# A decoder layer of Trainium2: the order of its first transfers and products, where its resident weights land, and what paces the mixers' steps

## The chip, the cores and the metric

The kernel runs on one core of one Trainium2 chip. The metric is device time in microseconds (us) of that core, as the median of several runs. Beside it stands one profiled execution, which the trace describes instruction by instruction.

## The reference

One layer of a decoder trunk, for 256 tokens (T), a width D of 2048 and a batch of 1, all in float32:

```python
mod = silu(c) @ w_ada + b_ada                    # 6 x D: shift, scale, gate of both halves
h = rmsnorm(x) * (1 + sc1) + sh1
proj = h @ w_in                                  # pool u | q,k,v | gla q,k,v,r,a | 3 x D gate logits
y_pool = pool(u); y_sb = stick_breaking(q, k, v) # 4 windows; 8 heads of 128
y_gla = gla(...)                                 # 4 heads, decay from a
y = sum_i sigmoid(g_i) * (y_i @ w_br_i)
x = x + ga1 * (y @ w_out)
h = rmsnorm(x) * (1 + sc2) + sh2
x = x + ga2 * ((silu(h @ w_gate) * (h @ w_up)) @ w_down)
```

## The kernel before

Everything is held transposed: channels on the 128 partitions, tokens along the free axis, so D is 16 blocks of 128. A tile framework puts in the semaphores and chooses, from its own estimates, the order in which each engine's instructions are issued; instructions may move ahead of earlier ones unless an edge forbids it.

**Products.** Matmuls run on float32r operands. A float32 factor is split into a rounded float32r part, hi, and a rest, lo: ACT casts hi (L113), DVE subtracts to get lo (L114), in parts of `PART` = 1024 columns (768 for some). `mm3` makes hi·hi, hi·lo and lo·hi (L128 to L130); token-major pieces do the same at L342. A plain float32 product is two passes of the array and far slower per column; it is used where an operand isn't split (L309, the mixers, the start).

**Buffers.** `wraw` has four raw buffers of 128 x 2048 float32 (`raw`), into which SP loads, in one queue, everything heavy: weights (`load`, L94) and rows of w_ada (`ada_vec`, L227). `wsplit` has three buffers for hi and lo. `slots` has 61 tiles of 128 x 512 float32 (`slot`) for everything else. PSUM has four banks `acc` and four `mx`.

**Vectors.** A column of `mod` is the dot product of c and a 1 MB block of w_ada: `ada_vec` lets DVE multiply and add (L230) against `cs`, which is silu(c) spread over all partitions by four products (L215) with a one-hot matrix `oh`.

**Stage 1, start.** SP loads x in four tiles, ACT squares them, PE sums them over partitions by `c2048` products (L267), and `rsqrt` gives rstd. `keep_busy` (L206) runs products of zeros.

**Stage 2, blocks 0 to 15.** As soon as block n of h is known (`modulate`, two vectors a block), PE applies `persistent(n)`, 12 products into six resident banks (the first three head pairs' q and k), in plain float32 for n < 5 (L309) from weights in slots, and through `Weights` behind that; and `extra`, pieces of the other 16 column pairs for some blocks of h, each summed into a slot by ACT or DVE (L320, L322). From block 4 on every block has two such pieces of 1 MB.

**Stage 3, mixers.** 33 short chains (generators `stick_breaking`, `gla_level`, `pool` and so on) are advanced in steps between the last pieces and then the gate projections (`gate`, `proj`: 48 of them, 48 products each). `steps(n)` advances up to n of the chains that are due by a `clock` that each call moves by a fixed cost; 30 gates (`LEAD`) come before the merge. `ada(n)` adds n to a running count and computes one vector for every 2 in it.

**Stage 4.** The merge of the branches, w_out, the second norm and SwiGLU, with `mm2` (a 512 and a 256 column product, L147, L148).

Of the kernel before, what the change touches and what calls it, by code (L numbers as in the profile page):

```python
# [8 lines left out]
F32 = mybir.dt.float32  # L9
# [5 lines left out]
P = 128  # L15
# [43 lines left out]
def kernel(ctx: ExitStack, tc: tile.TileContext, xT, c, vecs, consts, invc, masks, w_ada, w_per, w_ext,  # L59
                      w_gate, w_a1, w_a2, w_pool, w_br, w_out, w_ff, w_down, outT):  # L60
    nc = tc.nc
    mm = nc.tensor.matmul
    recent = deque(maxlen=6)
# [6 lines left out]

    vec = nc.vector

# [18 lines left out]
    def load(src):  # L91
        raw = wraw.tile([P, WW], F32, tag="raw", name=f"raw{next(names)}")
        n = src.shape[-1]
        nc.sync.dma_start(raw[:, :n], src)  # L94
        return raw[:, :n]

    def split_buffer(shift, n):
        t = wsplit.tile([P, 2 * PART + 128], F32R, tag="w", name=f"w{next(names)}")
        return t[:, shift:shift + n], t[:, shift + PART:shift + PART + n]

    class Weights:

        def __init__(self, src, part=PART, shift=SHIFT):
            self.raw, self.part, self.shift, self.made = load(src), part, shift, {}

        def at(self, col, n):
            i = col // self.part
            if i not in self.made:  # L110
                raw = self.raw[:, i * self.part:min((i + 1) * self.part, self.raw.shape[-1])]
                hi, lo = split_buffer(self.shift, raw.shape[-1])
                nc.scalar.copy(hi, raw)  # L113
                vec.tensor_tensor(lo, raw, hi.bitcast(F32), ALU.subtract)  # L114
# [75 lines left out]
    cz, oh, idle = slot()[:4, :], slot()[:4, :], slot()  # L190
    nc.scalar.dma_start(cz, c[0])
    nc.scalar.dma_start(oh, c[1])
    nc.scalar.preload_act_table_set("silu_and_others")
    vec.memset(idle, 0.0)
    for i in range(4):
        nc.sync.dma_start(xt[i], xT[:, 4 * i:4 * i + 4, :])
    nc.sync.dma_start(vt, vecs)
    c2048, c128, neg, eps = full(1.0 / D), full(1.0 / P), full(-1.0), full(EPS, 1)
# [24 lines left out]
    def ada_vec(t, parts=1):  # L223
        raw = wraw.tile([P, WW], F32, tag="raw", name=f"raw{next(names)}")
        w = D // parts
        for i in range(parts):
            nc.sync.dma_start(raw[:, i * w:(i + 1) * w], w_ada[t, :, i * w:(i + 1) * w])  # L227
# [29 lines left out]
    for i in range(4):  # L257
        sq = [slot(), slot()]
        for j in range(2):
            act(sq[j], xt[i][:, 2 * j:2 * j + 2, :].rearrange("p a t -> p (a t)"), AF.Square)  # L260
        if i < 2:
            vec.tensor_copy(*spread[2 * i])
        vec.tensor_tensor(sq[0], sq[0], sq[1], ALU.add)
        if i < 2:
            nc.scalar.copy(*spread[2 * i + 1])
        for j in range(2):
            mm(ms[:, :T], lhsT=c2048, rhs=sq[0][:, j * T:(j + 1) * T], start=i == 0 and j == 0,  # L267
               stop=i == 3 and j == 1)
    keep_busy(4)
    ada_vec(16, 2)  # L270
# [27 lines left out]
    def persistent(k):  # L298

        if k < NATIVE:  # L300
            w = [slot() for _ in range(3)]
            for i, wi in enumerate(w):
                nc.sync.dma_start(wi, w_per[k, :, i * 512:(i + 1) * 512])
# [22 lines left out]
    def extra(piece, bank):  # L326

        es, c0, c1 = EXT[piece][1:]
        n = (c1 - c0) * T
        w = Weights(w_ext[piece, :, :n * len(es)], 768 if n == 768 else PART)  # L330
        for i, e in enumerate(es):
# [261 lines left out]
    live = [0, 0]  # L593
    clock = [0]
    LEAD, LIVE, LAG, ST, ST2 = 30, 5, 1, 3, 2

    def unfinished():
        return bool(chains or lines[0] or lines[1])

    def steps(n, cost=5.2):  # L600
        clock[0] += cost
        for i, line in enumerate(lines):
            while line and live[i] < LIVE:
                chains.append([0, line.popleft(), i])
                live[i] += 1
        done = 0
        for e in sorted(chains, key=lambda e: e[0]):
            if done >= n or e[0] > clock[0]:
                break
            try:  # L610
                v = next(e[1])
                e[0] = clock[0] + (1 if v == "idle" else (v or 5) * LAG)
                done += v != "idle"
            except StopIteration:
                chains.remove(e)
                done += 1
# [7 lines left out]
    raw = load(w_a1)  # L624
    hi = split_buffer(0, 768)[0]
# [22 lines left out]

    def gate(due):

# [10 lines left out]
        sigs.append(s)  # L661
        ada(due)
        if unfinished():
            steps(ST)

    for n in range(LEAD):
        gate(0 if n < 10 else 1.4)
    while unfinished():
        steps(ST)
    assert raw  # L670
# [8 lines left out]
    for j in range(NK):  # L679
        while len(sigs) < min(3 * NK, LEAD + -(-(j + 1) * (3 * NK - LEAD) // NK)):  # L680
            gate(1.3)
        sig = sigs[3 * j:3 * j + 3]
# [12 lines left out]
        merged.append(split_x(m[:, :T]))  # L695
        ada(1.3 if j < NK - 2 else 0)

# [223 lines left out]
```

## Time and profile before

| | us |
|---|---|
| median of 3 runs | 1555.23 |
| lowest, highest | 1554.32, 1555.28 |
| profiled execution, its own time | 1558.11 |
| span of its trace, first to last instruction | 1556.3 |

The granted clock of TensorE is 0.992 of the full 2.4 GHz over the span. PE is busy for 1524.4 us of it, DVE for 1134.2, ACT for 733.2; these are sums over stages with different limits, and the sections below go by stretches of time. Times in a trace count from its first instruction.

### The profile page before, as it was taken

What the parts mean: (1) busy time and instruction counts of PE and PEld (TensorE: products, weight loads), DVE (VectorE), ACT (ScalarE), POOL (GpSimd) and SP (SyncE); (2) the same over time, 40 slices, a digit from 0 to 9 for tenths busy, and PEclk for the clock granted to TensorE, in tenths of its full rate; (3) what the DMA queues carried; (4) which work ended last, traced back from release to release, by engine and by line L of the source; (5) the groups of instructions that cost most, each with busy time, mean ns of one, the idle gap of its engine ahead of it and who ended that gap; (6) DMA issues with size and microseconds to landing.
All of it is one profiled execution on the core that took longest, in us unless ns stands there. A gap on an engine that the chain in (4) does not pass through costs nothing.

```text
span 1556.3 us, 25106 instructions
## 1 busy us (share of the span) xinstructions
PE 1524.4 (98%) x10376; PEld 1399.8 (90%) x10376; DVE 1134.2 (73%) x1515; ACT 733.2 (47%) x1020; POOL 9.8 (1%) x28
## 2 busy tenths in 40 slices
PE   8999999889999999999999999999999999999999
PEld 5899999779999999999889888888888888888888
DVE  5788887996896788888999666666666555545443
ACT  4334334745566444444556444544444444433333
POOL 0000000000000000001000000000000000000000
PEclk9999999989999999999999999999999999999999
DMA  8988887544667888887875666667666555556562
GB/s 331 365 297 299 299 287 250 185 156 163 222 233 261 314 300 315 303 308 286 293 276 173 243 246 215 245 244 244 217 245 246 189 190 186 192 197 206 184 206 85
DMA packets 58882, 377.30 MB, mean 242 GB/s; under 512 B 6536, under 2 KB 9992, under 8 KB 17424
## 3 DMA queue, kind: packets, MB, share of 16 engines
q1 hardware_dynamic: 58752, 375.68, 68.1%
q8 instruction: 81, 1.33, 0.3%
q14 instruction: 33, 0.27, 0.0%
q10 hardware_dynamic: 16, 0.02, 0.0%
HBM read 373.58 MB, written 2.10 MB: 241 GB/s over the span
## 4 chain that ended last, share of the span: by engine, by line
PE 87%; DVE 6%; DMA 4%; issue 1%; ACT 1%; SPq 0%; ACTq 0%; DVEq 0%
PE acc L147 33%; PE acc L148 16%; PE acc L128 9%; PE acc L130 9%; PE acc L129 8%; DMA raw<-in_w_ada_dram 2%; DVE raw L230 2%; PE mx L342 2%; PE mx L128 1%; PE mx L130 1%; PE mx L129 1%; DVE w L114 1%; PE acc L309 1%; PE acc L752 1%; PE acc L750 1%
## 5 line engine op out<-in xcount | busy, mean ns | idle before, releaser
L114 DVE TENSOR_TENSOR w<-raw,w 128x1024 fp32r<-128x1024 f32 (+2 forms) x520 | 618.9, 1192 | 291.5 <-ACT w L113 288.0
L113 ACT CAST w<-raw 128x1024 fp32r<-128x1024 f32 (+2 forms) x520 | 531.9, 1024 | 513.2 <-PE acc L148 241.7
L147 PE MATMUL acc<-s,w 128*128 128x512 f32 x2212 | 767.0, 393 | 0.0
L148 PE MATMUL acc<-s,w 128*128 128x256 f32 x2212 | 614.5, 278 | 0.0
L147 PEld LDWEIGHTS acc<-s,w 128*128 128x128 f32 x2212 | 415.0, 188 | 95.3
L148 PEld LDWEIGHTS acc<-s,w 128*128 128x128 f32 x2212 | 415.9, 188 | 0.0
L130 PE MATMUL acc<-s,w 128*128 128x256 f32 x1224 | 344.8, 282 | 8.2 <-DVE w L114 8.2
L128 PE MATMUL acc<-s,w 128*128 128x256 f32 x1224 | 348.8, 285 | 0.2 <-DVE s L322 0.2
L129 PE MATMUL acc<-s,w 128*128 128x256 f32 x1224 | 344.2, 281 | 0.0
L130 PEld LDWEIGHTS acc<-s,w 128*128 128x128 f32 x1224 | 233.0, 190 | 9.1 <-DVE w L114 9.0
L230 DVE CUSTOM_DVE_ANT_0 raw<-raw,cs,vt 128x2048 f32<-128x2048 f32 (+1 forms) x96 | 223.1, 2325 | 16.1 <-DMA raw<-in_w_ada_dram 15.9
L128 PEld LDWEIGHTS acc<-s,w 128*128 128x128 f32 x1224 | 232.5, 190 | 1.9 <-issue 1.0
L129 PEld LDWEIGHTS acc<-s,w 128*128 128x128 f32 x1224 | 232.1, 190 | 1.4 <-issue 1.2
L66 ACT ACTIVATE s<-s 128x256 f32<-128x256 f32 (+3 forms) x169 | 84.3, 520 | 33.6 <-DVE s L792 16.2
L128 PE MATMUL mx<-s,w 128*128 128x256 f32 x312 | 88.7, 284 | 6.2 <-DVE s L322 6.2
L791 ACT COPY s<-acc 128x256 f32<-128x256 f32 x82 | 30.6, 373 | 136.1 <-PE acc L148 136.1
L129 PE MATMUL mx<-s,w 128*128 128x256 f32 x312 | 87.8, 281 | 0.0
L130 PE MATMUL mx<-s,w 128*128 128x256 f32 x312 | 87.7, 281 | 0.0
L792 DVE TENSOR_TENSOR s<-s,acc 128x256 f32<-128x256 f32 x82 | 34.5, 420 | 52.9 <-ACT s L791 52.9
L128 PEld LDWEIGHTS mx<-s,w 128*128 128x128 f32 x312 | 59.3, 190 | 7.2 <-ACT w L113 5.9
L342 PE MATMUL mx<-w,s 128*128 128x256 f32 x492 | 59.8, 280 | 4.3 <-DVE s L322 1.9
L342 PEld LDWEIGHTS mx<-w,s 128*128 128x128 f32 x492 | 57.8, 188 | 5.5 <-ACT w L113 2.4
(153 smaller groups left out, 932.6 us busy)
## 6 DMA issues: line engine op xcount, KB each, us to landing
raw<-in_w_ada_dram SPq DMA_DIRECT2D x94, 1024.0 KB, 5.1
raw<-in_w_ff_dram SPq DMA_DIRECT2D x88, 1024.0 KB, 4.9
raw<-in_w_gate_dram SPq DMA_DIRECT2D x48, 1024.0 KB, 5.0
raw<-in_w_down_dram SPq DMA_DIRECT2D x32, 1024.0 KB, 5.0
raw<-in_w_ext_dram SPq DMA_DIRECT2D x29, 1024.0 KB, 5.9
raw<-in_w_br_dram SPq DMA_DIRECT2D x16, 1024.0 KB, 5.4
raw<-in_w_out_dram SPq DMA_DIRECT2D x16, 1024.0 KB, 4.9
raw<-in_w_down_dram SPq DMA_DIRECT2D x16, 768.0 KB, 4.2
```

What stands on the lines that cost most here:

```text
L66: r = nc.scalar.activation(out, in_, func, **kw)
L113: nc.scalar.copy(hi, raw)
L114: vec.tensor_tensor(lo, raw, hi.bitcast(F32), ALU.subtract)
L128: mm(out, lhsT=wh, rhs=x[:, :T], start=first, stop=False, skip_group_check=True)
L129: mm(out, lhsT=wh, rhs=x[:, T:], start=False, stop=False, skip_group_check=True)
L130: mm(out, lhsT=wl, rhs=x[:, :T], start=False, stop=last, skip_group_check=True)
L147: mm(out, lhsT=wh, rhs=x, start=first, stop=False, skip_group_check=True)
L148: mm(out[:, :T], lhsT=wl, rhs=x[:, :T], start=False, stop=last, skip_group_check=True)
L230: vec.tensor_tensor_reduce(p, p, cs[:, i * w:(i + 1) * w], 1.0, mod_col(t) if i else vt[:, V_ADA + t:V_ADA + t + 1], ALU.mult, ALU.add, mo ...
L342: mm(o, lhsT=l, rhs=r, start=first and j == 0, stop=last and j == 2, skip_group_check=True)
L791: nc.scalar.copy(o, m[:, T:])
L792: vec.tensor_tensor(o, o, m[:, :T], ALU.add)
```

## The change

It does five things.

1. **Pinned order.** Loads go through `fetch`, which holds a transfer behind the previous one of its queue, in the first three blocks (`pinned`); the first products (idle ones, spreading, mean) are held in program order on PE by `in_order`. c comes through SP instead of ACT. The idle products are placed anew: one of 256 columns after each mean step, nine more before the first block.
2. **c spread as hi and lo.** GpSimd rounds the one-hot matrix, ACT casts c to hi, DVE makes lo, and eight float32r products take the place of four float32 ones. The first two squared tiles are no longer added, but summed by four products.
3. **Resident weights via slots.** w_per of the blocks from 5 on and the first three pieces are loaded as 256 KB tiles into slots, not into a raw buffer; `Weights` splits them 512 columns at a time.
4. **Mixers' steps by a sum of work.** `mm` adds an estimate of its time to `given["pe"]`, every DVE instruction (with a margin of 6%) to `given["dve"]`. `steps()` advances the chain that has been due longest, as long as DVE's sum is no more than `AHEAD` = 1 us before PE's; DVE's sum may fall no more than `BEHIND` = 4 us behind. Gates are made until the chains are done, so `LEAD` follows.
5. **Vectors likewise.** In the mixers and the merge, a vector is computed only when the sum leaves room after the steps and while more than 23 are left.

```diff
+    given = {"pe": 0.0, "dve": 0.0, "margin": 1.06}
+    def mm(out, lhsT, rhs, **kw):
+        n = 1
+        for d in rhs.shape[1:]:
+            n *= d
+        given["pe"] += n * (0.00046 if rhs.dtype == F32R else 0.00168)
+        return nc.tensor.matmul(out, lhsT=lhsT, rhs=rhs, **kw)
...
+    class Vec:
...
+                given["dve"] += (0.13 + n * 0.00107) * given["margin"]
...
+    def fetch(dst, src):
+        r = nc.sync.dma_start(dst, src)
+        if pinned[0]:
+            tc.keep_in_program_order(r)
...
+    def load_slots(src):
+        raw = [slot() for _ in range(src.shape[-1] // 512)]
+        for i, r in enumerate(raw):
+            fetch(r, src[:, i * 512:(i + 1) * 512])
+        return raw
...
+                while lo_c < hi_c:
+                    m = min(hi_c - lo_c, w - lo_c % w)
+                    raw, c = self.raw[lo_c // w][:, lo_c % w:lo_c % w + m], lo_c - i * self.part
+                    nc.scalar.copy(hi[:, c:c + m], raw)
+                    vec.tensor_tensor(lo[:, c:c + m], raw, hi[:, c:c + m].bitcast(F32), ALU.subtract)
+                    lo_c += m
...
-    nc.scalar.dma_start(cz, c[0])
-    nc.scalar.dma_start(oh, c[1])
-    nc.scalar.preload_act_table_set("silu_and_others")
+    fetch(cz, c[0])
+    first = nc.scalar.dma_start(oh, c[1])
+    with tc.issue_after(first.ins):
+        nc.scalar.preload_act_table_set("silu_and_others")
...
-    keep_busy(2, T)
+    for _ in range(2):
+        keep_busy(1, T)
     silu = act(cz, cz, AF.Silu)
+    ohr, chi, clo = (slot(F32R)[:4, :] for _ in range(3))
+    nc.gpsimd.tensor_copy(ohr, oh)
+    nc.scalar.copy(chi, cz)
     with tc.issue_after(silu.ins):
         nc.scalar.preload_act_table_set("natural_log_exp_and_others")
-    spread = []
-    for i in range(4):
-        m = mx()
-        mm(m, lhsT=oh[:, i * P:(i + 1) * P], rhs=cz, start=True, stop=True)
-        spread.append((cs[:, i * 512:(i + 1) * 512], m))
+    vec.tensor_tensor(clo, cz, chi.bitcast(F32), ALU.subtract)
+    spread = [(cs[:, i * 512:(i + 1) * 512], mx()) for i in range(4)]
+    for part in (chi, clo):
+        for i in range(4):
+            in_order(spread[i][1], lhsT=ohr[:, i * P:(i + 1) * P], rhs=part, start=part is chi, stop=part is clo)
...
-        if i < 2:
-            vec.tensor_copy(*spread[2 * i])
-        vec.tensor_tensor(sq[0], sq[0], sq[1], ALU.add)
...
+        if i:
+            vec.tensor_tensor(sq[0], sq[0], sq.pop(), ALU.add)
...
+        for t in sq:
+            for j in range(2):
+                in_order(ms[:, :T], lhsT=c2048, rhs=t[:, j * T:(j + 1) * T], start=i == 0 and t is sq[0] and j == 0,
+                         stop=i == 3 and j == 1)
+        keep_busy(1, T)
+    keep_busy(9, T)
...
-            w = Weights(w_per[k], 768)
+            w = Weights(w_per[k], load=load_slots)
...
+        w = Weights(w_ext[piece, :, :n * len(es)], 768 if n == 768 else PART, load=load_slots if piece < 3 else load)
...
+        pinned[0] = n < 3
...
+    LIVE, AHEAD, BEHIND = 5, 1.0, 4.0
...
+    def steps():
+
+        given["dve"] = max(given["dve"], given["pe"] - BEHIND)
+        while True:
...
+            e = min(chains, key=lambda e: e[0], default=None)
+            if e is None or e[0] > given["pe"] or given["dve"] > given["pe"] + AHEAD:
                 break
             try:
                 v = next(e[1])
+                e[0] = given["pe"] + (2.5 if v == "idle" else v or 5)
...
+        while len(ada_q) > 16 + 7 and given["dve"] + 2.4 < given["pe"] + AHEAD:
+            ada(2)
...
         for e in extra(pieces.popleft(), acc):
-            ada(0.625)
-            steps(ST2, 2.6)
+            steps()
...
-    for n in range(LEAD):
-        gate(0 if n < 10 else 1.4)
     while unfinished():
-        steps(ST)
+        gate()
+    LEAD = len(sigs)
+    given["margin"] = 1.0
...
-        ada(1.3 if j < NK - 2 else 0)
+        steps()
```

## Rows read from the trace of the kernel before

**Rows 1.** Windows of seven stretches; columns: stretch, length, busy us (count) of PE, PEld, DVE, ACT, POOL, clock, DMA.

```profile
24.80:31.00 6.20, 6.16 (x15) 4.94 (x16) 5.30 (x7) 3.31 (x4) 0.00 (x0) 0.51 0.61 207
31.00:90.00 59.00, 57.21 (x386) 53.30 (x385) 47.13 (x56) 23.77 (x38) 0.61 (x2) 1.00 0.91 352
90.00:276.00 186.00, 176.93 (x1488) 174.07 (x1488) 156.49 (x186) 74.45 (x87) 0.00 (x0) 0.99 0.80 287
276.00:345.00 69.00, 57.09 (x364) 49.40 (x363) 67.07 (x131) 42.51 (x69) 0.71 (x2) 0.93 0.47 164
345.00:500.00 155.00, 155.00 (x1251) 150.97 (x1251) 122.24 (x195) 92.57 (x154) 0.34 (x1) 0.99 0.62 220
500.00:820.00 320.00, 320.00 (x2493) 310.25 (x2492) 273.97 (x375) 145.52 (x193) 7.37 (x16) 1.00 0.82 295
820.00:1556.30 736.30, 733.07 (x4357) 647.15 (x4355) 450.84 (x551) 340.61 (x461) 0.00 (x0) 1.00 0.61 209
```

**Rows 2.** Whom PE waited for, whole run; columns: us in total, times, longest.

```profile
PE acc L130 <- DVE w L114: 8.2, 4, 3.4
PE mx L128 <- DVE s L322: 6.2, 4, 1.9
```

**Rows 3.** DVE groups by line, 108.38 to 208.29 us: busy, mean ns, idle before.

```profile
L114 DVE TENSOR_TENSOR w<-raw,w 128x1024 fp32r<-128x1024 f32 (+1 forms) x36 | 40.5, 1133 | 4.8 <-ACT w L113 4.8
L230 DVE CUSTOM_DVE_ANT_0 raw<-raw,cs,vt 128x2048 f32<-128x2048 f32 x12 | 28.2, 2349 | 6.4 <-DMA raw<-in_w_ada_dram 6.4
```

**Rows 4.** Windows of six blocks, and of a stretch without PE waits.

```profile
108.38:208.29 99.91, 93.70 (x803) 92.85 (x803) 87.15 (x102) 38.83 (x43) 0.00 (x0) 1.00 0.85 302
180.00:200.00 20.00, 20.00 (x174) 20.00 (x173) 18.49 (x24) 7.22 (x8) 0.00 (x0) 1.00 0.93 336
```

**Rows 5.** What SP's transfers waited for, 108.38 to 208.29 us.

```profile
SPq L94 <- DVE w L114: 46.2, 18, 3.5
SPq L227 <- DVE mod L230: 41.1, 12, 5.7
```

**Rows 6.** DVE groups, 276 to 345 us and, last two, 345 to 500.

```profile
L114 DVE TENSOR_TENSOR w<-raw,w 128x1024 fp32r<-128x1024 f32 (+1 forms) x12 | 13.6, 1132 | 0.0
L230 DVE CUSTOM_DVE_ANT_0 raw<-raw,cs,vt 128x2048 f32<-128x2048 f32 x4 | 9.4, 2348 | 0.0
L322 DVE TENSOR_TENSOR s<-s,acc 128x512 f32<-128x512 f32 x14 | 9.4, 683 | 0.0
...
L114 DVE TENSOR_TENSOR w<-raw,w 128x1024 fp32r<-128x1024 f32 x45 | 54.8, 1223 | 16.8 <-ACT w L113 16.8
L230 DVE CUSTOM_DVE_ANT_0 raw<-raw,cs,vt 128x2048 f32<-128x2048 f32 x10 | 23.5, 2348 | 1.1 <-DMA raw<-in_w_ada_dram 0.9
```

**Rows 7.** Timeline of the start; columns: start us, us, engine line operation, what ended the idle time.

```profile
3.57 1.28 ACT L211 ACT_TABLE_LOAD   x1
...
4.75 7.16 PE L215 MATMUL mx<-s,s 4*128 4x512 f32 x8 [1.22 <-DMA s<-in_c_dram]
...
11.84 2.08 PE L267 MATMUL acc<-s,full 128*128 128x256 f32 x4
...
15.41 2.80 PE L267 MATMUL acc<-s,full 128*128 128x256 f32 x8
...
18.90 1.03 PE L267 MATMUL acc<-s,full 128*128 128x256 f32 x4
...
20.03 0.47 ACT L66 ACTIVATE s<-acc,full 128x256 f32<-128x256 f32 x1 [5.42 <-PE acc L267]
...
24.84 3.78 PE L309 MATMUL acc<-s,s 128*128 128x256 f32 x8 [3.19 <-ACT s L66]
```

**Rows 8.** Transfers of 33 to 60 us and, last line, of 90 to 270.

```profile
DMA packets 2090, 10.58 MB, mean 392 GB/s; under 512 B 225, under 2 KB 225, under 8 KB 993
...
s<-in_w_per_dram SPq DMA_DIRECT2D x9, 256.0 KB, 6.8
...
DMA packets 8194, 51.74 MB, mean 287 GB/s; under 512 B 912, under 2 KB 1168, under 8 KB 3260
```

More of the change, by code (lines that the diff above doesn't have):

```diff
@@ L69, in act, with __getattr__, call @@
         return r
-    vec = nc.vector
+    class Vec:
+        def __getattr__(self, name):
+            op = getattr(nc.vector, name)
+            def call(out, *a, **kw):
+                n = 1
+                for d in out.shape[1:]:
+                    n *= d
+                given["dve"] += (0.13 + n * 0.00107) * given["margin"]
+                return op(out, *a, **kw)
+            return call
+    vec = Vec()
+    pinned = [True]
+    def fetch(dst, src):
+        r = nc.sync.dma_start(dst, src)
+        if pinned[0]:
+            tc.keep_in_program_order(r)
     const = ctx.enter_context(tc.tile_pool(name="const", bufs=1))
@@ L93, in load @@
         n = src.shape[-1]
-        nc.sync.dma_start(raw[:, :n], src)
-        return raw[:, :n]
+        fetch(raw[:, :n], src)
+        return [raw[:, :n]]
+    def load_slots(src):
[3 more added lines that the diff above has]
+        return raw
     def split_buffer(shift, n):
@@ L101, with __init__ @@
     class Weights:
-        def __init__(self, src, part=PART, shift=SHIFT):
+        def __init__(self, src, part=PART, shift=SHIFT, load=load):
             self.raw, self.part, self.shift, self.made = load(src), part, shift, {}
@@ L110, in at @@
             if i not in self.made:
[L111 to L114, printed above, removed]
+                w = self.raw[0].shape[-1]
+                lo_c, hi_c = i * self.part, min((i + 1) * self.part, w * len(self.raw))
+                hi, lo = split_buffer(self.shift, hi_c - lo_c)
+                while lo_c < hi_c:
[4 more added lines that the diff above has]
+                    lo_c += m
                 self.made[i] = hi, lo
@@ L226, in ada_vec @@
         for i in range(parts):
-            nc.sync.dma_start(raw[:, i * w:(i + 1) * w], w_ada[t, :, i * w:(i + 1) * w])
+            fetch(raw[:, i * w:(i + 1) * w], w_ada[t, :, i * w:(i + 1) * w])
         for i in range(parts):
@@ L260 @@
             act(sq[j], xt[i][:, 2 * j:2 * j + 2, :].rearrange("p a t -> p (a t)"), AF.Square)
-        if i < 2:
-            vec.tensor_copy(*spread[2 * i])
-        vec.tensor_tensor(sq[0], sq[0], sq[1], ALU.add)
[L264 to L269, printed above, removed]
+        if i:
+            vec.tensor_tensor(sq[0], sq[0], sq.pop(), ALU.add)
+        if i == 0:
+            for j in range(2):
+                vec.tensor_copy(*spread[j])
+        if i == 1:
+            for j in range(2, 4):
+                nc.scalar.copy(*spread[j])
+        for t in sq:
+            for j in range(2):
+                in_order(ms[:, :T], lhsT=c2048, rhs=t[:, j * T:(j + 1) * T], start=i == 0 and t is sq[0] and j == 0,
+                         stop=i == 3 and j == 1)
+        keep_busy(1, T)
+    keep_busy(9, T)
     ada_vec(16, 2)
@@ L300, in persistent @@
         if k < NATIVE:
-            w = [slot() for _ in range(3)]
-            for i, wi in enumerate(w):
-                nc.sync.dma_start(wi, w_per[k, :, i * 512:(i + 1) * 512])
+            w = load_slots(w_per[k])
         else:
-            w = Weights(w_per[k], 768)
+            w = Weights(w_per[k], load=load_slots)
         for t in range(12):
@@ L593 @@
     live = [0, 0]
-    clock = [0]
-    LEAD, LIVE, LAG, ST, ST2 = 30, 5, 1, 3, 2
+    LIVE, AHEAD, BEHIND = 5, 1.0, 4.0
     def unfinished():
         return bool(chains or lines[0] or lines[1])
[L600 to L608, printed above, removed]
+    def steps():
+        given["dve"] = max(given["dve"], given["pe"] - BEHIND)
+        while True:
+            for i, line in enumerate(lines):
+                while line and live[i] < LIVE:
+                    chains.append([0, line.popleft(), i])
+                    live[i] += 1
+            e = min(chains, key=lambda e: e[0], default=None)
+            if e is None or e[0] > given["pe"] or given["dve"] > given["pe"] + AHEAD:
                 break
@@ L611, in steps @@
                 v = next(e[1])
-                e[0] = clock[0] + (1 if v == "idle" else (v or 5) * LAG)
-                done += v != "idle"
+                e[0] = given["pe"] + (2.5 if v == "idle" else v or 5)
             except StopIteration:
                 chains.remove(e)
-                done += 1
                 if len(e) == 3:
                     live[e[2]] -= 1
+        while len(ada_q) > 16 + 7 and given["dve"] + 2.4 < given["pe"] + AHEAD:
+            ada(2)
     def proj(n):
         return block([w_gate[n]], h)
-    raw = load(w_a1)
+    raw = load(w_a1)[0]
     hi = split_buffer(0, 768)[0]
@@ L647, with gate @@
     sigmoid = [None]
-    def gate(due):
+    def gate():
         r = proj(len(sigs))
@@ L695 @@
         merged.append(split_x(m[:, :T]))
-        ada(1.3 if j < NK - 2 else 0)
+        steps()
     with tc.issue_after(sigmoid[0].ins):
```

17 lines of the change are left out of this document (7 added, 10 removed).

## The prediction

> **What bounds the kernel now.** I began with the windows of the whole run, because a busy share alone hides where the waits lie. From 345 us on the matmul engine is idle for 3.2 us of 1211, all in the last stretch, at the full clock or within 1% of it [rows 1]: nothing that the diff does to DVE, ACT or the queues there can shorten it. So the change is worth what is lost before 345 us. For each stretch I take its length less PE's busy time, plus the length times the missing share of the clock (PE's records overlap, so very short waits are not seen). 24.8 to 31 us: 3.0 us, nearly all of it clock (0.51 granted). 31 to 90 us: 1.8. 90 to 276 us: 9.1 idle and 1.9 of clock, 11.0. 276 to 345 us: 11.9 idle and 4.8 of clock, and 1.6 more of clock just behind it, 18.3. Together 34.1 us; ahead of them stand 24.8 us before the first useful product.
>
> Then I asked who ends the waits. In the long middle stretch PE waits for DVE's additions into the piece sums (L322), in the stretch after it for DVE's low halves of the weights (L114) [rows 2]. These are two different shortages. In the middle DVE is at 87.2 of 99.9 us and itself waits 6.4 us for vector rows of w_ada and 4.8 us for ACT's casts [rows 3, 4]; and SP stands still 87.3 of 99.9 us until a raw buffer is free [rows 5]. A transfer leaves only when one of the four raw buffers comes back. From 276 to 345 us, instead, DVE waits for almost nothing: 67.1 of 69.0 us busy [rows 1], and of this only 23.0 us are what PE needs next (13.6 splits, 9.4 additions); 9.4 us are four vectors that nobody needs yet, the other 35 us mixer steps [rows 6].
>
> **Start.** The four spreading products are fp32, two passes each, eight passes in 7.16 us at the low clock [rows 7]. The change makes eight fp32r passes of 512 columns. A pair of 512 and 256 columns takes 2 x 736.3 / 4357 = 0.338 us at the full clock [rows 1], a 256-column product 20.0 / 174 = 0.115 [rows 4], so 512 columns cost 0.223 and twice that, 0.45, at the low clock: 3.6 us, 3.6 less. Against that an ACT cast stands ahead of the first product (by the nearest row, a DVE addition of 512 columns, 0.68 [rows 6]); the low half's subtraction, another 0.68, is hidden by the first four products, the GpSimd copy of the one-hot rows by Silu. If the table load of 1.28 us [rows 7] goes ahead of the cast, the products begin at about 5.5, else at 4.2, and end between 7.8 and 9.1 instead of 11.9. But the products now stand in a written order, and that order has ten mean products (two passes of 0.43 at the low clock, 8.5 us) and three idle ones between them (2.6): 11.1 us at the low clock, where the old order took from 11.9 to 19.9. In the old run four mean passes from 11.84 us take 2.08 us and four from 18.90 take 1.03; the eight from 15.41 lie between, so the clock rose about there [rows 7]. Taken the same here, 3.6 to 4.9 us of slow work are left then, 1.8 to 2.5 us at full speed, and the mean is done at 17.2 to 17.9, 2.0 to 2.7 earlier. From there to the first product it is 4.8 us [rows 7], and the half vector that DVE computes inside that chain may or may not move out. I take **2.5 us**; bounds 1.0 (cast late, half vector kept) and 4.5 (clock up sooner, half vector gone).
>
> **Clock behind it.** Before, PE sat idle for 3.2 us ahead of L309 and then ran 16 passes at the low clock [rows 7, 1]. Now ten idle products stand in that gap, 4.3 us at the full clock against a chain of 3.6 to 4.8. I take **3.0 us**, all of the loss; 1.5 if half of it comes back.
>
> **31 to 90 us.** The pinned transfers put the weights of block 0 ahead of the vectors of block 1, and nothing pinned waits for a raw buffer, since w_per and pieces 0 to 2 leave the ring. Blocks 0 to 2 need about 3.9 MB each, at 392 GB/s [rows 8] 10 us, PE some 10.8: the transfers keep up, barely. I take **1.0 of 1.8 us** (0 to 1.8). Pieces of 512 columns make four splits of 0.68 out of two of 1.22, 0.3 us of DVE per piece, hidden by the fifth of this stretch in which DVE is free [rows 1].
>
> **90 to 276 us.** Six blocks take 99.9 us, 16.65 each [rows 4]. PE's own work is 132 products of 0.115 us, 15.2. DVE is busy 14.5 per block, 14.65 with three splits of 0.68 for the old two (1.90), and 0.8 goes to ACT waits: 15.45. So neither forces 16.65; the 1.07 us per block that DVE waits for w_ada does, and behind DVE's queue the L322 additions that free PE's banks. The ring now serves four loads a block instead of five: at its present turn-round (4 buffers, 5 loads, 16.65 us: 13.3 us a buffer) it would allow a block in 13.3 us. The bound becomes DVE's 15.45 to 15.6, 1.0 less, over 11 blocks 11. DVE would then be at 94% with waits in its queue, so I take **6.5 us**; bounds 2.0 (the ring was only the first of several waits) and 11.0 (all of it). SP's extra issues (three of 0.4 us for one) go into its 87 us of waiting.
>
> A rule of the Trainium skill speaks against this part: "DMA: Bandwidth & Descriptors", section Bandwidth, asks for 1 MiB or more per DMA and fits one transfer as 2.0 us plus its bytes over 436 GB/s. The 768 KB weight cut in three would by that estimate take 4 us more of a queue that has 12.7 us of work a block, 16.7 in all, and the 6.5 us would be gone: 1535. The trace speaks otherwise: in 33 to 60 us nine loads are such 256 KB pieces, and this stretch moves 392 GB/s, against 287 in 90 to 270 us [rows 8].
>
> **Mixers, 276 us on.** Until now two steps are released per projected column pair, whatever they cost. The new sum counts PE 0.118 us per 256 columns and DVE 1.30 us per 1024-column split (the trace has 0.115 and 1.22), and releases a step only while DVE's sum is less than 1 us ahead; it starts at most 4 us behind, so some 5 us of steps come at once and the rest as room arises. Vectors come last, so the four of 9.4 us leave this stretch. What must be done, 23 us of splits and additions against 240 products, 28 us, of PE work in the last pieces, then fits. The steps move behind the gate projections: a gate is 48 products, 5.5 us, with 2.4 us of splits, 3.1 us of room. Mixer work is 67.1 - 32.4 = 35 us in one stretch and 122.2 - 54.8 - 23.5 = 44 in the next [rows 1, 6], so some 25 gates hold it, no more than the 30 of before. I take **14 of 18.3 us**; bounds 6 and 18.3. The vectors that leave come later, where PE has never waited.
>
> **Sum.** 2.5 + 3.0 + 1.0 + 6.5 + 14 = 27.0 us off the profiled 1556.3 (1558.1 with what lies around it; 2.9 above the median of the runs). From the median 1555.2: **1528**. The bounds add to 10.5 and 38.6; all at one end is unlikely, so the case's own range is 1517 to 1541.
>
> **Rivals.** (a) *The mixers keep their loss.* DVE's work is the same, only later; if casts and steps still queue ahead of the splits, the 14 us stay: 1542. For it: DVE at 0.97 in one stretch and 0.79 in the next leaves 189 of 224 us busy [rows 1], little to spread. Against: PE was never late at 0.79. (b) *The transfers do not get faster.* If loads keep to 287 GB/s with the ring open, a block's 4.98 MB takes 17.4 us, 0.7 more than now: 8 us lost, the 6.5 not won, 1542. This is where the page's rule would end, with a mechanism of its own; rows 8 speak against it. (c) *Slower.* The sum holds DVE just under full through all the mixers. If that makes PE wait as it did in 276 to 345 us (16.7 of 69.0 us, 24%) over the 165 us that the last pieces and 25 gates take, 40 us are lost there instead of 18.3, and 13 won elsewhere: 1564. It decides from 31 us on, 19% of those 165. Against it: the price of a step counts 6% above the trace. (d) *Nothing.* The order of issue comes out much as before, since the scheduler had already put early work first: within 3 us of 1555.
>
> **Chances.** Forecast 0.62, (a) 0.18, (b) 0.04, (c) 0.10, (d) 0.06. Faster by over 0.2% (3 us, about what a measurement of this kernel can tell): 0.62 + 0.18 + 0.04 = 0.84; within it 0.06; slower 0.10. The range 1517 to 1549 takes in (a) and (b) and leaves out (c), (d) and thin tails.
>
> **What would show it.** First L309 product at about 22 us, at the full clock, no granted 0.5 behind it. Blocks at 15.5 to 16 us, few DVE waits for w_ada, SP no longer waiting nine tenths. No window of 276 to 345 us with DVE above 0.97 and PE idle; no vectors there. It is wrong if PE's waits for L114 return further on, or if DVE, freed of w_ada, waits for casts instead.

## The result and the profile after

The changed kernel takes **1535.34 us** (median of 4 runs, 1534.12 to 1537.35) against 1555.26 for the kernel before in the same session (1554.32 to 1558.0): a ratio of 0.987 with an interval of 0.9853 to 0.9887. That is 19.9 us less; the prediction was 1528, 27 less, range 1517 to 1549. The profiled execution has a span of 1532.3 us (own time 1534.12), 24.0 less than the 1556.3 of before. Of the 4 us between 24.0 and 19.9, 2.9 are before's profile above its median and 1.2 after's below its own.

Three marks of the two traces divide the 24.0 us completely: the first product of block 5, the first of block 15, and the first transfer of w_ff, from which it is 758.5 us to the end in both.

| stretch | before | after | won | predicted |
|---|---|---|---|---|
| to block 5 | 85.5 | 79.5 | 6.0 | 6.5 |
| blocks 5 to 15 | 165.1 | 153.2 | 11.9 | 6.5 |
| block 15 to w_ff | 547.2 | 541.1 | 6.1 | 14 |
| w_ff to the end | 758.5 | 758.5 | 0.0 | 0 |

The predicted 6.5 us of the first row are the terms for the start, the clock behind it and the stretch up to 90 us (2.5 + 3.0 + 1.0).

The windows of the changed kernel answer to [rows 1]; columns as there. Every matmul now has line L70, every DVE instruction of the wrapper L88, most activations L74, casts of weights L150, transfers L96.

```profile
24.80:31.00 6.20, 6.20 (x35) 5.48 (x34) 6.14 (x9) 2.31 (x6) 0.00 (x0) 1.00 1.05 424
31.00:90.00 59.00, 58.65 (x414) 55.63 (x414) 48.86 (x63) 26.96 (x45) 0.00 (x0) 1.00 0.91 344
90.00:276.00 186.00, 186.00 (x1581) 182.79 (x1580) 171.42 (x220) 83.04 (x108) 0.62 (x2) 1.00 0.85 307
276.00:345.00 69.00, 68.97 (x534) 64.87 (x533) 55.07 (x97) 44.57 (x71) 0.53 (x1) 1.00 0.48 159
345.00:500.00 155.00, 149.35 (x1194) 144.36 (x1194) 127.79 (x222) 95.89 (x164) 0.53 (x1) 0.98 0.55 196
500.00:820.00 320.00, 314.22 (x2434) 302.05 (x2433) 286.97 (x399) 148.91 (x200) 8.39 (x16) 1.00 0.84 304
```

In the first four stretches, PE's idle time and slow clock are gone but for 0.4 us. In the last two, where it had no idle time before, it now has 5.65 and 5.78 us. The waits of the whole run, which answer to [rows 2], name what ends them: ACT's casts and, as before but in another place, DVE's low halves.

```profile
PE acc L70 <- ACT w L150: 6.6, 2, 5.5
PE acc L70 <- DVE w L88: 4.6, 5, 1.4
```

**Where the 5.5 us lie.** The timeline of the changed kernel from 455 us on (columns as in [rows 7]) shows one wait (`...` stands for lines left out):

```profile
455.72 1.28 ACT L74 ACT_TABLE_LOAD   x1
457.01 4.54 ACT L74 ACTIVATE s<-s 128x512 f32<-128x512 f32 x13
...
462.06 3.08 ACT L74 ACTIVATE s<-s 128x512 f32<-128x512 f32 x9
...
465.64 1.03 ACT L74 ACTIVATE s<-s 128x256 f32<-128x256 f32 x3
...
466.83 2.93 ACT L150 CAST w<-raw 128x1024 fp32r<-128x1024 f32 x3
...
467.92 6.31 PE L70 MATMUL acc<-s,w 128*128 128x256 f32 x31 [5.50 <-ACT w L150]
```

When the mixers are done, ACT loads the sigmoid's table and applies it to all the gates held back; the casts of the next weights stand behind this row of sigmoids. In the kernel before, casts broke the same row off, and PE waited for none of them (columns as above, its own timeline):

```profile
477.74 0.94 ACT L66 ACTIVATE s<-s 128x256 f32<-128x256 f32 x2
478.59 1.03 ACT L113 CAST w<-raw 128x1024 fp32r<-128x1024 f32 x1
479.52 1.33 ACT L66 ACTIVATE s<-s 128x256 f32<-128x256 f32 x4
```

In the changed kernel the granted clock falls in PE's pause and stays low behind it; the window of the same trace:

```profile
466.00:473.00 7.00, 4.93 (x22) 4.64 (x23) 5.39 (x7) 3.76 (x7) 0.00 (x0) 0.53 0.69 217
```

PE is busy for 4.93 us of this stretch at about half the clock, which by our estimate loses another 2.4. This one place takes 7.9 us. With the 5.8 us of waits from 500 us on, 13.7 of the 18.3 us that were lost before are lost again further on; that leaves 4.6, and the marks say 6.1 (idle time does not show all, see the last section).

**The start.** Timeline of the changed kernel, 3 to 26 us:

```profile
3.35 1.28 ACT L257 ACT_TABLE_LOAD   x1
...
4.64 0.62 ACT L255 CAST s<-s 4x512 fp32r<-4x512 f32 x1
...
5.40 3.75 PE L70 MATMUL mx<-s,s 4*128 4x512 f32 x8 [1.88 <-ACT s L255]
...
18.09 0.47 ACT L74 ACTIVATE s<-acc,full 128x256 f32<-128x256 f32 x1 [6.17 <-PE acc L70]
...
19.49 0.42 DVE L88 SCALAR_TENSOR_TENSOR s<-acc,s 128x256 f32<-128x256 f32 x1 [4.07 <-ACT s L74]
19.83 1.28 DVE L88 CUSTOM_DVE_ANT_0 raw<-raw,cs,vt 128x1024 f32<-128x1024 f32 x1
...
21.23 1.28 DVE L88 CUSTOM_DVE_ANT_0 raw<-raw,cs,mod 128x1024 f32<-128x1024 f32 x1
...
23.98 2.21 PE L70 MATMUL acc<-s,s 128*128 128x256 f32 x9 [1.67 <-ACT s L74]
```

The mean's root starts 1.94 us earlier than before (18.09 for 20.03 [rows 7]), but from there to the first product it is 5.89 us instead of 4.81: both half vectors of 1.28 us are in the chain, after DVE had stood idle for 4.07. Before, one of the two was done ahead of it. The first product comes 0.86 us earlier. Single profiles scatter here (last section): in the seven with this start the first product comes at 22.4 to 24.0 us, 23.4 in the mean, in the three with the old one at 23.5 to 24.8, 24.2 in the mean.

### The profile page after: what moved, and what is told of

Read it like the earlier page. It is cut to its first block, busy times and chain, and to the rows that moved or that the text cites. A ratio compares the mean times of both kernels' runs of the same rounds, so it can differ in the third digit from the quotient of the medians.

```text
span 1532.3 us, 25277 instructions
## 1 busy us (share of the span) xinstructions
PE 1512.3 (99%) x10398; PEld 1393.5 (91%) x10398; DVE 1136.0 (74%) x1532; ACT 737.3 (48%) x1040; POOL 11.4 (1%) x29
## 4 chain that ended last, share of the span: by engine, by line
PE 95%; DVE 2%; ACT 1%; DMA 1%; issue 0%; SPq 0%
PE acc L70 80%; PE mx L70 15%; DMA raw<-in_w_ada_dram 1%; ACT s L74 1%; DVE raw L88 1%; DVE w L88 1%; ACT w L150 0%; DVE s L88 0%; SPq L96 0%; ACT L74 0%; ACT s L160 0%; ACT s L369 0%; DVE x L88 0%; DVE mod L88 0%; DVE scl L88 0%
## 5 line engine op out<-in xcount | busy, mean ns | idle before, releaser
L70 PE MATMUL acc<-s,w 128*128 128x512 f32 (+2 forms) x8384 | 1247.4, 310 | 11.4 <-ACT w L150 6.6
L70 PEld LDWEIGHTS acc<-s,w 128*128 128x128 f32 x8384 | 1141.1, 188 | 113.4 <-ACT w L150 7.5
L88 DVE TENSOR_TENSOR w<-raw,w 128x1024 fp32r<-128x1024 f32 (+3 forms) x493 | 589.7, 1199 | 273.4 <-ACT w L150 269.3
L150 ACT CAST w<-raw 128x1024 fp32r<-128x1024 f32 (+1 forms) x492 | 506.7, 1033 | 463.7 <-PE acc L70 341.8
L88 DVE CUSTOM_DVE_ANT_0 raw<-raw,cs,vt 128x2048 f32<-128x2048 f32 (+1 forms) x96 | 223.0, 2323 | 6.1 <-DMA raw<-in_w_ada_dram 6.0
L70 PE MATMUL mx<-s,w 128*128 128x256 f32 (+1 forms) x952 | 116.8, 281 | 0.0
L70 PEld LDWEIGHTS mx<-s,w 128*128 128x128 f32 (+1 forms) x952 | 112.3, 187 | 2.3 <-ACT s L369 0.3
L74 ACT ACTIVATE s<-s 128x256 f32<-128x256 f32 (+3 forms) x171 | 85.4, 518 | 25.7 <-DVE s L88 23.9
L88 DVE TENSOR_TENSOR s<-s,s 128x256 fp32r<-128x256 f32 (+4 forms) x190 | 87.6, 465 | 9.6 <-ACT s L255 3.9
L88 DVE TENSOR_TENSOR s<-s,acc 128x256 f32<-128x256 f32 (+1 forms) x98 | 45.1, 463 | 54.5 <-ACT s L838 53.3
L70 PE MATMUL mx<-w,s 128*128 128x256 f32 x492 | 59.5, 279 | 0.0
L70 PEld LDWEIGHTS mx<-w,s 128*128 128x128 f32 x492 | 57.9, 188 | 0.5 <-DVE w L88 0.2
L70 PE MATMUL mx<-s,s 128*128 128x64 f32 (+5 forms) x276 | 50.3, 326 | 1.9 <-ACT s L255 1.9
L70 PEld LDWEIGHTS mx<-s,s 128*128 128x128 f32 (+1 forms) x276 | 39.8, 195 | 7.2 <-issue 4.5
L88 DVE TENSOR_TENSOR s<-s,mx 128x512 f32<-128x512 f32 (+2 forms) x57 | 37.5, 659 | 8.9 <-PE mx L70 7.6
L150 ACT CAST w<-s 128x512 fp32r<-128x512 f32 x45 | 26.0, 619 | 35.4 <-PE mx L70 32.3
L88 DVE TENSOR_TENSOR s<-s 128x256 f32<-128x256 f32 (+4 forms) x67 | 32.1, 478 | 3.5 <-PE mx L70 1.9
L88 DVE SCALAR_TENSOR_TENSOR x<-acc,mod,x 128x256 f32<-128x256 f32 x62 | 29.4, 479 | 6.7 <-PE acc L70 6.1
L88 DVE TENSOR_TENSOR w<-s,w 128x512 fp32r<-128x512 f32 x45 | 28.9, 685 | 1.2 <-ACT w L150 1.1
L74 ACT ACTIVATE s<-s,mod 128x256 fp32r<-128x256 f32 (+1 forms) x37 | 17.4, 504 | 21.1 <-DVE mod L88 15.2
```

The source lines that it names most:

```text
L70: return nc.tensor.matmul(out, lhsT=lhsT, rhs=rhs, **kw)
L74: r = nc.scalar.activation(out, in_, func, **kw)
L88: return op(out, *a, **kw)
L150: nc.scalar.copy(hi[:, c:c + m], raw)
```

## The experiments

All are compared with the kernel before. Each group of four ran in one session, so its medians compare directly; across groups, and with the changed kernel (0.987, 0.9853 to 0.9887), the ratios do. 0.001 of a ratio is 1.6 us; the intervals reach 2 to 5 us to either side, so that smaller differences between two kernels are not told by the ratios alone.

### One part taken back, or one alone

| kernel | median, us | ratio | interval |
|---|---|---|---|
| sums alone (parts 4, 5) | 1552.41 | 0.9972 | 0.996 to 0.9984 |
| old steps (parts 1, 2, 3) | 1539.05 | 0.9892 | 0.9872 to 0.9912 |
| ring for all (parts 1, 2, 4, 5) | 1539.62 | 0.9888 | 0.9863 to 0.9914 |
| old start (parts 3, 4, 5) | 1548.76 | 0.9953 | 0.9938 to 0.9968 |

**Sums alone.** The start (its lines are not shown), the pins and the slots as before:

```diff
-    pinned = [True]
+    pinned = [False]
...
-            w = Weights(w_per[k], load=load_slots)
+            w = Weights(w_per[k], 768)
```

> Only the sums of work for the mixers' steps and vectors are kept; start, transfers and weight buffers are as before. Theory (each part is worth what its own stretch shows): 18 us won in 276 to 365 us, 14 to 15 lost again at the sigmoids and in the merge: 1551 us. Rival (the late losses come only because the whole run is earlier and DVE fuller from the start): 1537 to 1540.

4.4 us less by the ratio: the theory held. PE is busy 69.00 of 69.00 us in 276 to 345 us, 149.32 of 155.00 behind it and 313.86 of 320.00 behind that: the sums do cure the stretch for which they were costed, and with the slow clock behind the first of these waits they hand about three quarters of its 18.3 us on.

**Old steps.** `ada` and `steps` by the old clock, all else as changed:

```diff
-            steps()
+            ada(0.625)
+            steps(ST2, 2.6)
...
-            gate()
+            gate(1.3)
```

> Start, pinned order and slots are kept; the steps and vectors go by the old clock. Theory: 0.9 + 3.0 at the start, 1.5 and 11.0 in the blocks, nothing won or lost behind them: 1539 us, with the old 12 us of idle time and low clock back behind the blocks. Rival (the sums are what wins): 1550 or more.

The theory held: PE is again busy only 55.49 of 69.00 us from 276 us on, at a clock of 0.95. Beside the other parts the sums are worth 3.4 us by the ratios, whose intervals overlap, and 4.6 by the marks (block 15 to w_ff in 545.7 us); not 14.

**Ring for all.** Weights of the blocks through the ring again, all else as changed:

```diff
-            w = Weights(w_per[k], load=load_slots)
+            w = Weights(w_per[k], 768)
...
-        w = Weights(w_ext[piece, :, :n * len(es)], 768 if n == 768 else PART, load=load_slots if piece < 3 else load)
+        w = Weights(w_ext[piece, :, :n * len(es)], 768 if n == 768 else PART)
```

> Everything as changed, but w_per and the first three pieces go through the four raw buffers again. Theory (the ring of raw buffers set the blocks' 16.65 us): the blocks go back to about 16.6 us, 1546 to 1548 us. Rival (the pinned order and the earlier start made the blocks faster): 1535 to 1538, blocks near 15.5 us.

Neither number was met; the rival is nearer. Only 2.8 us come back by the ratios, less than their intervals can tell. The trace is that of the slowest of the seven executions, 1554.63 us. Most of what it is above the median, 12.9 us, lies from w_ff on, where this kernel is the changed one; there PE runs without a pause, but does 2266 products where the changed kernel does 2310:

```profile
900.00:1300.00 400.00, 400.00 (x2266) 346.81 (x2265) 256.75 (x309) 195.32 (x284) 0.00 (x0) 1.00 0.63 220
```

So only its blocks are read here. 3 of the 10 from block 5 on take 16.3 us or more (up to 18.1), the others 15.0 to 15.7; together they take 158.8 us, 5.6 more than in the changed kernel. The ring, with five loads a block, was not what set 16.65 us in every block.

**Old start.** The start of before (its lines are not shown) and nothing pinned, with slots and sums:

```diff
-    pinned = [True]
+    pinned = [False]
...
-        pinned[0] = n < 3
```

> Slots and sums are kept; the start is as before and nothing is pinned. Theory: 0.9 us of start and 3.0 us of low clock are lost again, 1539 to 1541 us. Rival (the pinned order is also what feeds the blocks): 1545 or more, with PE idle between 31 and 90 us.

The rival held: 12.9 us lost by the ratio though the blocks load only four a block through the ring. They run at 15.1 to 19.2 us. Windows of this kernel:

```profile
31.00:90.00 59.00, 56.78 (x387) 53.03 (x386) 48.42 (x63) 26.27 (x44) 0.00 (x0) 1.00 0.92 361
90.00:276.00 186.00, 180.49 (x1515) 177.47 (x1514) 160.42 (x200) 77.94 (x101) 0.62 (x2) 0.99 0.80 285
```

Its DVE groups of the second window, beside those of the changed kernel's blocks 7 to 12 (110.20 to 202.20 us), which answer to [rows 3]; first this kernel:

```profile
L88 DVE TENSOR_TENSOR w<-raw,w 128x1024 fp32r<-128x1024 f32 (+2 forms) x50 | 58.5, 1174 | 10.2 <-ACT w L150 9.6
L88 DVE CUSTOM_DVE_ANT_0 raw<-raw,cs,vt 128x2048 f32<-128x2048 f32 x19 | 44.6, 2348 | 6.1 <-DMA raw<-in_w_ada_dram 5.9
```

then the changed one, with its window and its SP waits of the same stretch (for [rows 4, 5]):

```profile
L88 DVE CUSTOM_DVE_ANT_0 raw<-raw,cs,vt 128x2048 f32<-128x2048 f32 x13 | 30.5, 2346 | 0.0
L88 DVE TENSOR_TENSOR w<-raw,w 128x1024 fp32r<-128x1024 f32 x24 | 29.2, 1222 | 2.3 <-ACT w L150 2.2
```

```profile
110.20:202.20 92.00, 92.00 (x794) 91.44 (x793) 88.52 (x112) 38.38 (x48) 0.62 (x2) 1.00 0.91 329
```

```profile
SPq L96 <- DVE mod L88: 47.2, 12, 6.6
SPq L96 <- DVE w L88: 22.4, 12, 3.6
```

In these blocks of the changed kernel DVE never waits for a row of w_ada; with the old start it does, ring open (6.1 us above) or not (6.4 [rows 3]). Six blocks take 92.0 us, 15.33 each, and PE has no idle time left in them. The marks of the traces give a table of two by two:

| blocks 5 to 15, us | resident weights in the ring | in slots |
|---|---|---|
| old start | 165.1 (before), 163.7 (sums alone) | 161.4 (old start) |
| new start | 158.8 (ring for all) | 153.2 (changed kernel) |

Nine more profiles with the new start and slots have 153.0 to 154.0. So each of the two is worth something alone, the start more, and it takes both for 153. Two of the four cells rest on one trace. Whether the written order or the earlier time carries more of the start's share was not told apart.

### The new waits: three edits alone and together

| kernel | median, us | ratio | interval |
|---|---|---|---|
| sigmoids later | 1532.89 | 0.9841 | 0.9818 to 0.9865 |
| fewer vectors in the merge | 1549.54 | 0.9951 | 0.9931 to 0.9971 |
| first sum ahead of the root | 1531.81 | 0.9837 | 0.9813 to 0.9861 |
| all three | 1541.72 | 0.991 | 0.9876 to 0.9944 |

**Sigmoids later.** `opened(n)` applies the sigmoid to the next n of the gates held back:

```diff
-        for s in raw:
-            sigmoid[0] = act(s, s, AF.Sigmoid)
+    opened(6)
...
+        opened(3 if j else 0)
```

> The stored gates' sigmoids, which the changed kernel runs in one piece on ACT behind the last exponential, are made for two merge steps at first and then three at each merge step. Theory (this burst holds up the casts of the next weights: 5.5 us of PE idle, then 6.8 us at the low clock): 8 to 9 us less than the changed kernel, 1526 to 1528 us, no wait of PE near 462 us. Rival (the merge's own start is what PE waits for): the wait only moves, 1533 to 1536.

The wait went: in this kernel's timeline ACT's row breaks off for two casts,

```profile
457.40 3.00 ACT L74 ACTIVATE s<-s 128x512 f32<-128x512 f32 x8
460.31 1.98 ACT L150 CAST w<-raw 128x1024 fp32r<-128x1024 f32 x2
```

but the waits for DVE's low halves grew from 4.6 us to

```profile
PE acc L70 <- DVE w L88: 8.2, 10, 1.6
```

so a part of the 7.9 us was lost again: 4.5 us are won by the ratios, 2.1 by the marks of the two traces (block 15 to w_ff in 539.0 us), where the theory had 8 to 9. The rival was right in kind: PE waits in the merge for some of what it no longer waits at 462 us.

**Fewer vectors.**

```diff
-    given["margin"] = 1.0
+    given["margin"] = 1.12
...
-        while len(ada_q) > 16 + 7 and given["dve"] + 2.4 < given["pe"] + AHEAD:
+        if len(ada_q) > 16 + 7 and given["dve"] + 2.4 < given["pe"] + AHEAD:
```

> At most one vector at each call, and in the merge a margin of 12% on DVE's sum instead of none. Theory (PE's waits for DVE's low halves from 620 to 720 us come from two vectors in a row, 2.4 us each, with a sum that has no margin): 5 to 6 us less, 1529 to 1531 us. Rival (DVE's work is just too much there): the waits stay or move on, 1534 to 1536.

A miss: slower than the changed kernel by 12.6 us by the ratios. 26 vectors instead of 34 are computed between 465 and 690 us, and what is left is flushed at w_out, where PE waits 15.6 us at once for casts behind it.

**First sum ahead of the root.**

```diff
-    keep_busy(9, T)
+    keep_busy(7, T)
     ada_vec(16, 2)
-    rstd = rsqrt(ms[:, :T])
+    last = ada_vec(0, 2)
+    with tc.issue_after(last.ins):
+        rstd = rsqrt(ms[:, :T])
...
-        ada_vec(k, 1 if k else 2)
+        if k:
+            ada_vec(k)
```

> The first shift vector's two halves are issued on DVE before the norm's steps instead of between them; two idle products fewer. Theory (both halves, 1.28 us each, stand in the chain from the mean to the first product while DVE idles 4.1 us ahead of it): first product at about 21.5 us instead of 24.0, 1532.5 to 1533.5 us. Rival (the first blocks wait for transfers anyway): the first product is earlier, the time stays at 1535.

The theory held, and the gain is above it, 5.1 us by the ratios for 2 to 3. Timeline of this kernel:

```profile
15.28 1.03 PE L70 MATMUL acc<-s,full 128*128 128x256 f32 x4
...
16.41 0.47 ACT L74 ACTIVATE s<-acc,full 128x256 f32<-128x256 f32 x1 [4.53 <-PE acc L70]
...
20.16 3.72 PE L70 MATMUL acc<-s,s 128*128 128x256 f32 x16 [0.40 <-ACT s L74]
```

From the root to the first product it is now 3.75 us for 5.89: 2.14 are the edit's. That the root itself starts 1.68 us earlier is not: with the changed kernel's own start it came as early, at 16.50 us, in the profile of the kernel with fewer vectors (the last section).

**All three.**

> The three edits together. Theory: 2.4 + 8.7 + 5.8 = 17 us less than the changed kernel, about 1518 us. Rival (the gains overlap, because DVE's and ACT's work only moves): 1524 to 1528.

Neither number was met: the vectors' edit costs here what it cost alone (one wait of 16.2 us at w_out).

### Is it the amount of DVE's work, or where a vector stands?

| kernel | median, us | ratio | interval |
|---|---|---|---|
| start and sigmoids | 1528.85 | 0.9821 | 0.9799 to 0.9842 |
| sixteen vectors fewer | 1527.46 | 0.9825 | 0.9793 to 0.9857 |
| sixteen fewer and sigmoids | 1522.47 | 0.9778 | 0.9759 to 0.9798 |
| start, sigmoids, one vector a call | 1522.49 | 0.9781 | 0.9761 to 0.9801 |

Sixteen fewer leaves out 16 columns of `mod`, which stay zero. Its edit:

```diff
-    ada_q = deque((*range(32, 48), *range(64, 80), *range(48, 64), *range(80, 96)))
+    ada_q = deque((*range(32, 48), *range(64, 80), *range(80, 96)))
+    nc.gpsimd.memset(mod[:, 48:64], 0.0)
```

that for one a call is the `if` of the miss above, without its margin, on top of the two good edits.

> The changed kernel with both edits that won alone: the sum over the first half vectors ahead of the root (3.5 us alone), and the gates' sigmoids in threes as the columns need them (2.4 us alone). If the two act in different places, they add: 1535.3 - 3.5 - 2.4 = about 1529.5. Rival: what is won at the start is waited for again in front of the merge, since VectorE ends late there whatever comes before: 1531 to 1533, PE's waits for VectorE's splits between 470 and 700 us growing beyond the 8.2 us that they were with the sigmoids' edit alone.

> Leaves out part of the computation: the 16 columns of w_ada with numbers 48 to 63 are not loaded and not summed, and their sums are set to zero; nothing else differs from the changed kernel. It takes 16 x 2.34 us = 37 us of VectorE's work and 16 transfers from the stretch before w_out. Theory, VectorE's whole work up to w_out is what makes its splits late in the merge: with 25 vectors instead of 41 the waits of 1.3 to 1.5 us between 620 and 700 us go (some 5 us of PE's idle time there), the wait for the gates' sigmoids at 462 us stays, and the time is 1529 to 1531. Rival, it is where a vector is placed (two in a row ahead of a column's split) and not how many there are: the waits stay as long as vectors are left, and the time is 1533 to 1536.

> The same 16 columns of w_ada left out (their sums are zero), and the gates' sigmoids in threes as the columns need them. Theory, VectorE's work is what took back the sigmoids' gain: with 37 us less of it the edit is worth the whole wait at 462 us and the slow clock behind it, 5.5 + 3.5 = some 8 us, so 8 below the kernel with 16 fewer alone: 1521 to 1523. Rival, something else takes it back: 2 to 3 us below it, 1527 to 1533.

> The kernel with the first sum ahead of the root and the sigmoids in threes, and in it at most one vector a call of the steps instead of as many as the running sums allow; the margin stays. Theory, the waits between 620 and 700 us come from two vectors in a row on VectorE ahead of a column's split: one a call takes them away without leaving more than a few vectors to the stage of w_out, so 2 to 5 us below the kernel with the two edits: 1525 to 1528. Rival, what one call doesn't issue the next does, or it is left over to w_out, where PE waits 15 us for it as with fewer vectors in the merge: 1530 to 1541.

The two good edits add within what can be told: 1528.85 for the 1529.5 of the theory; by the ratios 7.6 us together for 4.5 and 5.1 alone. Sixteen fewer gave 7.0 by the ratios (4 to 6 expected), and PE's waits for low halves, 4.6 us in the changed kernel, are gone from its list, as the theory of the amount had it. The windows of 620 to 700 us, first the changed kernel, then sixteen fewer:

```profile
620.00:700.00 80.00, 74.99 (x629) 74.17 (x628) 68.45 (x83) 31.51 (x41) 4.79 (x6) 1.00 0.91 332
```

```profile
620.00:700.00 80.00, 80.00 (x691) 79.30 (x690) 51.79 (x69) 36.06 (x45) 5.91 (x11) 1.00 0.60 210
```

But this does not part the amount from the place. Two vectors on DVE with no low half between them stand four times in 465 to 720 us of the changed kernel (from 625.8, 644.6, 663.3 and 681.5 us), and the only four waits of PE above 1 us in 500 to 720 us come 7 us behind them (at 633.0, 651.6, 670.2 and 688.4 us; 5.0 of the 5.8 us). Sixteen fewer has no such pair there. It also has 16 rows fewer to pass through the raw buffers: in 620 to 700 us the casts of the changed kernel wait 17.0 us for transfers of w_br and w_gate, in sixteen fewer for none.

On top of it the sigmoids' edit gave 5.0 us by the medians and 7.3 by the ratios (one of six runs of sixteen fewer took 1542.2 us and weighs on its ratio), between the theory's 8 and the rival's 3. Its window of 500 to 620 us shows that 1.9 us of waits come back even so, in the first part of the merge,

```profile
500.00:620.00 120.00, 118.11 (x995) 117.29 (x995) 97.18 (x124) 49.71 (x63) 0.00 (x0) 1.00 0.84 307
```

and with them two pairs of vectors, from 522.1 and 563.0 us. The longest of these waits stands behind the second:

```profile
562.97 2.35 DVE L88 CUSTOM_DVE_ANT_0 raw<-raw,cs,vt 128x2048 f32<-128x2048 f32 x1
...
566.11 2.34 DVE L88 CUSTOM_DVE_ANT_0 raw<-raw,cs,vt 128x2048 f32<-128x2048 f32 x1
...
570.11 2.15 PE L70 MATMUL acc<-s,w 128*128 128x256 f32 x16 [1.23 <-DVE w L88]
```

The two profiled executions are only 2.0 us apart (5.1 of idle time and 2.4 of slow clock won, 1.9 lost, 5.6); the other 3.6 are what is left over, and some 3 of pace, in the last section, are part of it. So less work for DVE alone does not keep the sigmoids' whole gain.

Place counts. The last kernel leaves nothing out and computes the same 34 vectors from 465 to 690 us, never two in one call, so that no such pair is left, and comes to 6.4 us below start and sigmoids, the same kernel without that edit (2 to 5 expected). The windows, first start and sigmoids, which has six pairs, then the last kernel:

```profile
620.00:700.00 80.00, 74.32 (x621) 72.97 (x620) 67.86 (x85) 32.64 (x40) 7.72 (x10) 1.00 0.88 326
```

```profile
620.00:700.00 80.00, 76.80 (x637) 75.30 (x636) 71.34 (x87) 33.67 (x42) 6.94 (x10) 1.00 0.89 333
```

The low halves in the same stretch, in the last kernel and in the changed one:

```profile
L88 DVE TENSOR_TENSOR w<-raw,w 128x1024 fp32r<-128x1024 f32 x28 | 33.5, 1218 | 2.0 <-ACT w L150 1.9
```

```profile
L88 DVE TENSOR_TENSOR w<-raw,w 128x1024 fp32r<-128x1024 f32 x27 | 32.6, 1221 | 10.9 <-ACT w L150 10.9
```

Two vectors in a row hold the low halves for 4.7 us; then DVE, with no time to spare, stands idle for the next casts, 10.9 us in this stretch (9.7 in start and sigmoids). One at a time, it is 2.0. Idle time of DVE alone does not make PE wait: sixteen fewer has 25.4 us of it here. The changed kernel's timeline shows such a pair, with only small operations between, and PE waiting behind it:

```profile
625.83 2.34 DVE L88 CUSTOM_DVE_ANT_0 raw<-raw,cs,vt 128x2048 f32<-128x2048 f32 x1
...
628.96 2.34 DVE L88 CUSTOM_DVE_ANT_0 raw<-raw,cs,vt 128x2048 f32<-128x2048 f32 x1
...
631.69 2.35 DVE L88 TENSOR_TENSOR w<-raw,w 128x1024 fp32r<-128x1024 f32 x2
...
632.96 7.22 PE L70 MATMUL acc<-s,w 128*128 128x256 f32 x59 [1.34 <-DVE w L88]
```

Three waits of 1.0 to 1.1 us stay in the last kernel without a pair; whether they go with the amount was not tried.

The last kernel, 1522.49 us, is the best complete version: 0.9% below the changed one by the ratios. In its trace block 15 to w_ff takes 530.9 us (230.2 to 761.1), 16.3 less than before: the 14 us that the prediction put on the mixers were there, but the change alone reached only 6.1.

## Why the prediction was right, and where it was off

**The sign, the range, and what bounds the kernel** were right: all that was won came from before 345 us, and the end, 758.5 us from w_ff on, did not move. That the sum came as near as 24.0 for 27.0 us is in part luck: the blocks gave 5.4 us more than forecast and the mixers 7.9 less.

**Start, 2.5: too high, 0.86,** a little below its bound. The root came 1.94 us earlier (2.0 to 2.7 predicted), the cast behind the table load, as its late case had it. The bound of 1.0 named the reason, a half vector kept in the chain; there were two.

**Clock behind it, 3.0: right.** The granted clock of 24.8 to 31 us is 1.00 for 0.51. **31 to 90 us, 1.0:** 1.4 (idle time 1.79 to 0.35).

**Blocks, 6.5: too low, 11.9, and the reason was half of one.** The step "the ring now serves four loads a block instead of five" is not the cause by itself: with five loads and the new start most blocks run at 15.0 to 15.7 us, with four and the old start many are slow (up to 19.2). What the term left out is the start, which is worth more in these blocks than the slots. Nor is DVE's 15.45 us the next bound: at 15.33 us a block it is PE itself that is full (92.00 of 92.00 us). The weighing of the 256 KB pieces held: with them the blocks take 15.33 us, and with the weights in one transfer again the kernel was not faster (2.8 us slower by the ratios, within their intervals). The cut by itself was not tried: that kernel took back the buffer with it. The rule of the Trainium skill, "DMA: Bandwidth & Descriptors", section Bandwidth, is 1 MiB or more per DMA; the fit that the prediction joins to it stands on the same page under "Anatomy of one DMA — SWDGE (gpsimd) path" and is for transfers issued by GpSimd, where these are issued by SP. The prediction's estimate by that fit would have put the blocks at 16.7 us; they are shorter, and the measurement decides.

**Mixers, 14: too high, 6.1, the step that failed.** The stretch itself behaved as predicted: PE 68.97 of 69.00 us, DVE 0.80, no vector from 276 to 345 us. What failed is "the vectors that leave come later, where PE has never waited" and, beside it, the sigmoids of the held-back gates, for which the prediction has no term at all. The first brought the 5.8 us of waits from 500 us on (34 vectors from 465 to 690 us for 25 before, some two in a row), which the prediction named as its refutation ("if PE's waits for L114 return further on"); the second the 7.9 us at 462. Rival (c) put such waits into the mixers themselves, 40 us of them. There none came; in the merge, where the same sum releases the vectors, they are 5.8 us.

## What to carry to other kernels

A pause moved off one stretch must be costed where it lands: ask, for each engine, what row of instructions is now in front of the next cast or low half. Here work without a due time cost least in one piece at a time between pieces that have one, and holding more of it back cost more than spreading it. And test a queue's explanation of a slow stretch from both ends: open the queue alone, and leave it closed with everything else changed.

## What the hardware showed that was not expected

The pace of the first products rises at a different time in each run. In the eleven profiles with the new start, the products up to 11 us begin within 0.1 us of each other, and from 5.4 us until the mean is done PE runs without a pause. Yet two idle products take 1.06 us in the changed kernel at 12.65 and 0.59 us in the kernel with the first sum ahead of the root at 12.26:

```profile
12.65 1.06 PE L70 MATMUL acc<-s 128*128 128x256 f32 x2
```

```profile
12.26 0.59 PE L70 MATMUL acc<-s 128*128 128x256 f32 x2
```

The mean is then done at 16.3 us there and 18.0 us here, the ends of the eleven: 1.7 us of difference that no edit made (16.4 with the changed kernel's own start, in fewer vectors). The clock column of a window there reads 1.00 for both, so it is the products' own durations that tell. A gain of a few us at the start has to be read from the stretch behind that rise.

And there are two paces at the full clock. In 640 to 660 us PE runs the same kind of product without a pause in both kernels with sixteen vectors fewer; the one without the sigmoids' edit does 179 of them, the one with it 172, as the kernel before does in the same window:

```profile
640.00:660.00 20.00, 20.00 (x179) 20.00 (x178) 12.73 (x19) 8.53 (x12) 0.00 (x0) 1.00 0.59 198
```

```profile
640.00:660.00 20.00, 20.00 (x172) 20.00 (x172) 11.62 (x16) 8.50 (x11) 0.18 (x1) 1.00 0.54 190
```

4% of pace, with the clock at 1.00 and the transfers alike. The changed kernel has the faster pace too, in 580 to 600 us (179), and not in most of the merge. Over the 80 us from 620 on sixteen fewer makes 691 products against the 665 of the other, some 3 us. The 12.9 us that the profile of ring for all lost from w_ff on are of this kind, 2266 products for 2310 in 400 us. What sets the pace was not tried; the sums above can be off by a few us for it.
